# A decoder layer with split weights: which engine makes the low parts of two down-projection pieces

## The chip, the cores and the metric

The kernel runs on one core of a Trainium2 chip. A core has a matrix engine (TensorE; PE in the rows, PEld for its weight loads), three engines for elementwise work (VectorE or DVE, ScalarE or ACT, GpSimd or POOL), a queue that issues loads (SyncE or SP), and 16 DMA engines that move data between the main memory and the core's own memory. Every engine works through its own list of instructions strictly in the order in which they were written; an instruction that waits holds up all that stand behind it on its engine.

The metric is the time of one execution on the device in microseconds (us): the median of the runs.

## The reference

One layer of a hybrid decoder on 256 tokens of width 1024: attention and a convolution module side by side, an output projection with a residual sum, then a SwiGLU feed-forward block with 2816 hidden units. Only the last block matters here:

```python
h = rms_norm(x, norm2_g[l])
x = x + (jax.nn.silu(h @ w_gate[l]) * (h @ w_up[l])) @ w_down[l]
```

All numbers are float32.

## The kernel before

**Weights.** All weights come in blocks of 128 x 2048 numbers (1 MB each, `raw` in the rows), one load each, through four buffers: a block is loaded when the last reader of an earlier block has released a buffer. A block is cut into pieces of 128 x 1024. TensorE multiplies in a shorter format, so each piece is split in a high part `wh`, made by ScalarE's rounding copy (L265), and a low part `wl`, the rest. The rest is made in one of two ways (`low_part`, L213): VectorE subtracts the high part from the block (L219); or, for the pieces in the list `BY_DMA`, ScalarE copies the high part with its sign turned (L216) and GpSimd issues a DMA that adds the piece, read from main memory a second time, onto that copy (L217). The parts live in eight slots, which are reused in turn.

**Down-projection.** The 22 row blocks of `w_down` form 11 pairs, one weight block each (blocks 36 to 46). Three pairs are plain and have two pieces each, straight from the block. The other eight go through a seven-product scheme for 2 x 2 matrices: VectorE forms sums `t` of the block's quarters (three instructions, L234 to L236), three pieces are split (the first from the block, the other two from `t`), and a quarter of the block is split by itself (`single`, L255: the high half `b11h` or `other` on ScalarE at L200, the low half `b11l` or `other` on VectorE at L201). In what follows the fast pairs count from 0: sum `t4` belongs to block 41, `t5` to 42, `t6` to 44, `t7` to 45; block 43 is the plain pair with the pieces 92 and 93, block 46 the last plain pair with 100 and 101.

| block | kind | pieces |
|---|---|---|
| 42 (`t5`) | fast | 89 from the block, 90 and 91 from `t5` |
| 43 | plain | 92, 93 |
| 44 (`t6`) | fast | 94 from the block, 95 and 96 from `t6` |
| 45 (`t7`) | fast | 97 from the block, 98 and 99 from `t7` |
| 46 | plain | 100, 101 |

**Products.** TensorE (L933) takes the pairs in order. For a fast pair it multiplies three times for each of seven products: high by high, low of the other factor by high, high by low of the weight. For the pairs of `t5` and `t6` it starts with the two products on the first piece (89, 94), goes on with the one on the single quarter, and ends with those on the second and third piece. For `t7` the product on the quarter comes first and piece 97 stands near the end.

**What sets the order.** `feed(upto)` (L261) is called ahead of each group of products. It first makes the high parts of as many pieces as a look-ahead allows, in the order of the list `turns`, and then the low parts, in the order of piece numbers, of all pieces up to `upto`. `turns` sorts the pieces by number, but a piece of the table `BEHIND` stands right behind the piece named there; so it is made early, since its adding DMA takes longer. The sums `t` of a block are written in front of the first piece that needs them.

Of the kernel before, what the change touches and what calls it, by code (L numbers as in the profile page):

```python
# [61 lines left out]
FAST = [p for p in range(NF // 2) if PAIRS[p] == "F"]  # L62
PLAIN = [p for p in range(NF // 2) if PAIRS[p] == "P"]
DOWN = 72
BEHIND = {75: 70, 78: 72, 81: 75, 82: 78, 86: 80, 89: 83, 92: 86, 93: 89, 97: 92}
BY_DMA = [*range(45, DOWN, 3), *BEHIND]
FAR = 46
SUMS = {66: 0, 69: 1}
# [73 lines left out]
def _build(nc, tc, t, ctx):  # L142
# [82 lines left out]
    index = {d: DOWN + a for a, d in enumerate(down)}  # L225
    turns = sorted(range(DOWN + len(down)), key=lambda j: BEHIND[j] + 0.5 if j in BEHIND else j)
    wsums, b11 = {}, {}
# [837 lines left out]
```

## Time and profile before

| | us |
|---|---|
| median of 3 runs (291.07 to 292.76) | 291.73 |
| the profiled execution, its own time | 292.81 |
| its span, from the first instruction to the last | 291.0 |
| TensorE busy | 282.4 |
| VectorE busy | 234.9 |
| ScalarE busy | 203.5 |
| GpSimd busy | 44.4 |

The mean granted clock of TensorE was 0.994. How to read the rows of the profile further down: a row of the timeline has the start (us from the start of the span), the duration, engine, line, operation, what it writes and reads (tile numbers left out), the shapes and a count; in brackets how long its engine had been idle just before and which instruction ended that. A row of the chain has start, duration and the instruction that held the end back in that stretch. Rows of DMA issues end with the time from the issue to the landing of the data. Rows of windows have busy times by engine in a stretch of the span, then the granted clock of TensorE (PEclk, 1.00 is full), the share of DMA engines in use, and GB/s.

### The profile page before, as it was taken

The page shows a single profiled execution, that of the slowest core. Times are in us where ns is not written, and L with a number is a line of the kernel's source. Part 1 is how long each engine was busy: PE and PEld are TensorE (multiplying, and loading weights), DVE is VectorE, ACT ScalarE, POOL GpSimd, SP SyncE. Part 2 cuts the span into 40 slices and gives each one's busy share as a digit, 9 for nine tenths or more (in the row PEclk, how much of TensorE's full clock was granted, in tenths as well). Part 3 has the DMA queues.
Part 4 walks back from the last instruction along what each step waited for, and adds up shares of the span by engine and source line. Part 5 has one row for each costly group of instructions (what it writes and reads, how often), then busy time and mean ns, then how long its engine had stood idle before and what let it go on. Part 6 is the DMA issues. An engine that isn't in the chain of part 4 may idle for free.

```text
span 291.0 us, 4146 instructions
## 1 busy us (share of the span) xinstructions
PE 282.4 (97%) x1466; PEld 236.2 (81%) x1466; DVE 234.9 (81%) x419; ACT 203.5 (70%) x332; POOL 44.4 (15%) x72
## 2 busy tenths in 40 slices
PE   8999999999999999999999999999999999997695
PEld 6888877788788888888888888888888888885484
DVE  4979995895976879999967868776698899948955
ACT  5866768996639674678878767877876798854640
POOL 0005473432000000000111011111111111201042
PEclk9999999999999999999999999999999999999799
DMA  7999868647013943564999999989966699994003
GB/s 252 406 423 379 356 233 291 238 144 278 13 57 131 384 152 107 196 268 164 298 251 324 281 293 239 289 248 294 204 190 200 177 306 206 238 338 101 0 0 144
DMA packets 13062, 66.14 MB, mean 227 GB/s; under 512 B 1713, under 2 KB 2321, under 8 KB 7410
## 3 DMA queue, kind: packets, MB, share of 16 engines
q1 hardware_dynamic: 10018, 55.14, 51.9%
q0 software_dynamic: 2880, 10.74, 19.0%
q8 instruction: 11, 0.18, 0.2%
q14 instruction: 9, 0.07, 0.1%
q10 hardware_dynamic: 144, 0.00, 0.0%
HBM read 64.83 MB, written 1.05 MB: 226 GB/s over the span
## 4 chain that ended last, share of the span: by engine, by line
PE 76%; DVE 12%; ACT 5%; DMA 3%; issue 2%; ACTq 0%; DVEq 0%
PE p L709 19%; PE fg L292 12%; PE fu L292 11%; PE po L755 8%; PE fg L294 6%; PE fu L294 6%; PE sum L933 5%; ACT wh L265 4%; DVE wl L219 4%; DMA raw<-w 3%; DVE t L234 3%; PE warm L354 1%; DVE t L235 1%; PE S L543 1%; DVE t L236 1%
## 5 line engine op out<-in xcount | busy, mean ns | idle before, releaser
L265 ACT ACTIVATE wh<-raw 128x1024 fp32r<-128x1024 f32 x82 | 85.0, 1053 | 18.9 <-PE fu L292 7.8
L219 DVE TENSOR_TENSOR wl<-raw,wh 128x1024 fp32r<-128x1024 f32 x64 | 77.1, 1220 | 8.6 <-ACT wh L265 8.5
L292 PE MATMUL fu<-g,wh 128*128 128x512 f32 x176 | 62.5, 395 | 0.0
L292 PE MATMUL fg<-g,wh 128*128 128x512 f32 x176 | 62.4, 394 | 0.0
L294 PE MATMUL fg<-g,wl 128*128 128x256 f32 x176 | 48.8, 277 | 0.0
L294 PE MATMUL fu<-g,wl 128*128 128x256 f32 x176 | 48.8, 277 | 0.0
L217 POOL DMA_DIRECT2D wl<-w x18 | 15.7, 875 | 179.8 <-PE fu L294 70.5
L292 PEld LDWEIGHTS fg<-g,wh 128*128 128x128 f32 x176 | 33.0, 187 | 7.7 <-DVE g L776 0.2
L292 PEld LDWEIGHTS fu<-g,wh 128*128 128x128 f32 x176 | 33.0, 188 | 7.6
L294 PEld LDWEIGHTS fg<-g,wl 128*128 128x128 f32 x176 | 33.1, 188 | 0.0
L294 PEld LDWEIGHTS fu<-g,wl 128*128 128x128 f32 x176 | 33.1, 188 | 0.0
L933 PE MATMUL sum<-wh,forms 128*128 128x512 f32 x84 | 26.8, 401 | 0.0
L709 PE MATMUL p<-wh,xh 128*128 128x512 f32 x80 | 26.2, 409 | 0.0
L709 PE MATMUL p<-wh,xl 128*128 128x512 f32 x80 | 25.0, 394 | 0.0
L709 PE MATMUL p<-wl,xh 128*128 128x512 f32 x80 | 24.7, 390 | 0.0
L265 ACT ACTIVATE wh<-t 128x1024 fp32r<-128x1024 f32 x16 | 16.9, 1055 | 9.9 <-DVE t L234 9.1
L219 DVE TENSOR_TENSOR wl<-t,wh 128x1024 fp32r<-128x1024 f32 x16 | 19.4, 1220 | 0.2
L216 ACT ACTIVATE wl<-wh 128x1024 fp32r<-128x1024 f32 x18 | 19.1, 1062 | 0.6
L933 PEld LDWEIGHTS sum<-wh,forms 128*128 128x128 f32 x84 | 16.4, 196 | 3.5
L709 PEld LDWEIGHTS p<-wh,xl 128*128 128x128 f32 x80 | 15.3, 191 | 3.4
L709 PEld LDWEIGHTS p<-wh,xh 128*128 128x128 f32 x80 | 14.5, 191 | 4.2 <-issue 1.0
L709 PEld LDWEIGHTS p<-wl,xh 128*128 128x128 f32 x80 | 15.1, 188 | 3.3
(203 smaller groups left out, 479.7 us busy)
## 6 DMA issues: line engine op xcount, KB each, us to landing
raw<-w SPq DMA_DIRECT2D x44, 1024.0 KB, 6.4
wl<-w POOLq DMA_DIRECT2D x18, 512.0 KB, 8.2
first<-first SPq DMA_DIRECT2D x8, 384.0 KB, 5.8
raw<-w SPq DMA_DIRECT2D x2, 512.0 KB, 6.6
xtok<-xtok SPq DMA_DIRECT2D x2, 512.0 KB, 9.1
x<-xtok SPq DMA_DIRECT2D x2, 512.0 KB, 6.8
c_rows<-rows SPq DMA_DIRECT2D x1, 768.0 KB, 10.6
out<-x SPq DMA_DIRECT2D x3, 256.0 KB, 2.0
```

Of the source, the lines that this page charges most:

```text
L216: nc.scalar.activation(dst[1], dst[0].bitcast(F32), AF.Copy, scale=-1.0)
L217: nc.gpsimd.dma_start(dst[1], src.bitcast(F32R), accum_op=ALU.add)
L219: nc.vector.tensor_tensor(dst[1], src, dst[0].bitcast(F32), op=ALU.subtract)
L234: nc.vector.tensor_tensor(u[:, 0:2 * W], w[:, 0:2 * W], w[:, W:3 * W], op=ALU.add)
L235: nc.vector.tensor_tensor(u[:, 2 * W:3 * W], u[:, 0:W], w[:, 2 * W:3 * W], op=ALU.add)
L236: nc.vector.tensor_tensor(u[:, 3 * W:], u[:, 2 * W:3 * W], w[:, 3 * W:], op=ALU.add)
L265: nc.scalar.activation(dst[0], src, AF.Copy)
L292: nc.tensor.matmul(out.rearrange("p (a q) -> p a q", a=2), w[0], both, start=z in first and z not in seen, stop=False)
L294: nc.tensor.matmul(out[:, 0:T], w[1], both[:, 0, :], start=False, stop=z in last and left[z] == 0)
L709: nc.tensor.matmul(banks[i], (xh, xh, xl)[a][:, kt, sls[i]], w[a % 2], start=kt == 0 and a == 0, stop=kt == KT - 1 and a == 1)
L755: nc.tensor.matmul(po[i, n], G["mix"][l][:, k, i * P:(i + 1) * P], w[r], start=k == a == 0, stop=k == KT - 1 and a == 2)
L933: nc.tensor.matmul(banks[m], lhs, rhs, start=first, stop=last)
```

## The change

```diff
-BEHIND = {75: 70, 78: 72, 81: 75, 82: 78, 86: 80, 89: 83, 92: 86, 93: 89, 97: 92}
+BEHIND = {75: 70, 78: 72, 81: 75, 82: 78, 86: 80, 89: 83, 92: 86}
 BY_DMA = [*range(45, DOWN, 3), *BEHIND]
```

`BEHIND` has two uses, and both change for the pieces 93 and 97. They are no longer in `BY_DMA`: VectorE subtracts for them, ScalarE's two copies with the sign turned and GpSimd's two DMAs of 512 KB each are gone. And in `turns` they stand at their own numbers. The end of the list was

```
92 87 88 93 90 91 97 94 95 96 98 99 100 101
```

and is now

```
92 87 88 90 91 93 94 95 96 97 98 99 100 101
```

Three places show what that moves. Names carry their numbers here (`wh97` is the high part of piece 97, `raw45` is block 45). First ScalarE, from the step behind `wh88` to the high half of the quarter of block 44. Before:

```order
L265 ACTIVATE wh93_2724<-raw43_2602 128x1024
L216 ACTIVATE wl93_2725<-wh93_2724 128x1024
L265 ACTIVATE wh90_2735<-t5_2737 128x1024
L200 ACTIVATE other_2522<-raw42_2581 128x512
L265 ACTIVATE wh91_2753<-t5_2737 128x1024
L265 ACTIVATE wh97_2766<-raw45_2709 128x1024
L216 ACTIVATE wl97_2767<-wh97_2766 128x1024
L265 ACTIVATE wh94_2777<-raw44_2667 128x1024
L265 ACTIVATE wh95_2787<-t6_2789 128x1024
L265 ACTIVATE wh96_2804<-t6_2789 128x1024
L265 ACTIVATE wh98_2814<-t7_2816 128x1024
L200 ACTIVATE b11h_1077<-raw44_2667 128x512
```

The same place now:

```order
L265 ACTIVATE wh90_2724<-t5_2726 128x1024
L265 ACTIVATE wh91_2738<-t5_2726 128x1024
L200 ACTIVATE other_2522<-raw42_2581 128x512
L265 ACTIVATE wh93_2752<-raw43_2602 128x1024
L265 ACTIVATE wh94_2764<-raw44_2667 128x1024
L265 ACTIVATE wh95_2774<-t6_2776 128x1024
L265 ACTIVATE wh96_2788<-t6_2776 128x1024
L265 ACTIVATE wh97_2801<-raw45_2709 128x1024
L265 ACTIVATE wh98_2811<-t7_2813 128x1024
L200 ACTIVATE b11h_1077<-raw44_2667 128x512
```

The high part of 97, which reads block 45, stood in front of those of 94, 95 and 96, which read block 44; it stands behind them now. The high part of 91 has moved in front of the high half of the quarter (`other`).

Second VectorE, behind the sum `t5`. Before:

```order
L219 TENSOR_TENSOR wl90_2736<-t5_2737,wh90_2735 128x1024
L201 TENSOR_TENSOR other_2522<-raw42_2581,other_2522 128x512
L219 TENSOR_TENSOR wl91_2754<-t5_2737,wh91_2753 128x1024
L219 TENSOR_TENSOR wl94_2778<-raw44_2667,wh94_2777 128x1024
L234 TENSOR_TENSOR t6_2789<-raw44_2667 128x1024
```

The same place now:

```order
L219 TENSOR_TENSOR wl90_2725<-t5_2726,wh90_2724 128x1024
L219 TENSOR_TENSOR wl91_2739<-t5_2726,wh91_2738 128x1024
L201 TENSOR_TENSOR other_2522<-raw42_2581,other_2522 128x512
L219 TENSOR_TENSOR wl93_2753<-raw43_2602,wh93_2752 128x1024
L234 TENSOR_TENSOR t6_2776<-raw44_2667 128x1024
```

The low half of the quarter of block 42 stands behind the low part of 91 now, and the low part of 93 has come in between. The low part of 94 has gone behind the sum `t6`.

Third VectorE, from the low part of 96 on. Before:

```order
L219 TENSOR_TENSOR wl96_2805<-t6_2789,wh96_2804 128x1024
L234 TENSOR_TENSOR t7_2816<-raw45_2709 128x1024
L235 TENSOR_TENSOR t7_2816<-t7_2816,raw45_2709 128x512
L236 TENSOR_TENSOR t7_2816<-t7_2816,raw45_2709 128x512
L201 TENSOR_TENSOR b11l_1078<-raw44_2667,b11h_1077 128x512
L219 TENSOR_TENSOR wl98_2815<-t7_2816,wh98_2814 128x1024
```

The same place now:

```order
L219 TENSOR_TENSOR wl96_2789<-t6_2776,wh96_2788 128x1024
L234 TENSOR_TENSOR t7_2813<-raw45_2709 128x1024
L235 TENSOR_TENSOR t7_2813<-t7_2813,raw45_2709 128x512
L236 TENSOR_TENSOR t7_2813<-t7_2813,raw45_2709 128x512
L219 TENSOR_TENSOR wl97_2802<-raw45_2709,wh97_2801 128x1024
L201 TENSOR_TENSOR b11l_1078<-raw44_2667,b11h_1077 128x512
```

The low part of 97 has come in ahead of the low half of the quarter of block 44 (`b11l`). TensorE's products stand in the same order as before. One more thing follows from the two DMAs: the load of block 46 waited for ScalarE (the last reader of block 43, the high part of 93), and now waits for VectorE (the last reader of block 42, the low half of its quarter).

## The prediction

> **What bounds the kernel now.** I read the page first, for the engine that is nearest to the whole span; then TensorE's timeline for its gaps; then the chain of waits, backwards from the largest gap.
>
> ```profile
> PE 282.4 (97%) x1466; PEld 236.2 (81%) x1466; DVE 234.9 (81%) x419; ACT 203.5 (70%) x332; POOL 44.4 (15%) x72
> ```
>
> TensorE is busy for 97% of the span, and its matmuls are the same before and after. So the change can only act through the few stretches in which TensorE waits or runs slowly. The timeline has one:
>
> ```profile
> 257.07 0.84 PE L933 MATMUL sum<-other,forms 128*128 128x512 f32 x3
> 257.75 0.62 PE L933 MATMUL sum<-wh,forms 128*128 128x512 f32 x2
> ...
> 267.14 0.39 PE L933 MATMUL sum<-wl,forms 128*128 128x512 f32 x1
> 272.09 1.00 PE L933 MATMUL sum<-b11h,forms 128*128 128x512 f32 x2 [4.56 <-ACT b11h L200]
> 272.89 0.72 PE L933 MATMUL sum<-b11l,forms 128*128 128x512 f32 x1
> ...
> 277.28 0.84 PE L933 MATMUL sum<-other 128*128 128x512 f32 x3
> ...
> 282.04 0.62 PE L933 MATMUL sum<-wh,act 128*128 128x512 f32 x2
> ```
>
> Three matmuls from 257.07 to 257.75 give a slot of 0.227 us each at full speed. After 267.14 the next could start at 267.37; it starts at 272.09, because the quarter of block 44 (`b11h`, `b11l`) was not split: 4.72 us lost. And the 15 matmuls from 272.09 to 277.28 take 5.19 us in place of 15 x 0.227 = 3.41, so 1.78 more. The second loss has its reason in the granted clock:
>
> ```profile
> 272.00:275.50 3.50, 3.41 (x8) 2.45 (x9) 3.43 (x4) 3.40 (x5) 0.00 (x0) 0.55 0.00 0
> 275.50:287.00 11.50, 11.50 (x55) 9.63 (x54) 7.78 (x11) 3.50 (x5) 5.12 (x4) 0.99 0.08 29
> ```
>
> 0.55 behind the gap, 0.99 afterwards. Together the place costs 6.50 us. The chain says what held it:
>
> ```profile
> 251.57 8.22 DMA raw<-w
> ...
> 259.88 1.07 ACT wh L265
> ...
> 261.94 1.05 ACT wh L265
> ...
> 263.01 1.23 DVE wl L219
> ...
> 268.01 1.23 DVE wl L219
> ...
> 270.46 1.06 ACT wh L265
> 271.52 0.53 ACT b11h L200
> ...
> 272.09 14.19 PE sum L933 x54
> ```
>
> The load issued at 251.57 is block 45 (it follows the release of block 41). ScalarE's next instruction needs it:
>
> ```profile
> 253.91 1.06 ACT L265 ACTIVATE wh<-t 128x1024 fp32r<-128x1024 f32 x1 [0.89 <-DVE t L234]
> 254.88 0.61 ACT L200 ACTIVATE other<-raw 128x512 fp32r<-128x512 f32 x1
> 255.40 1.05 ACT L265 ACTIVATE wh<-t 128x1024 fp32r<-128x1024 f32 x1
> 259.88 1.06 ACT L265 ACTIVATE wh<-raw 128x1024 fp32r<-128x1024 f32 x1 [3.44 <-DMA raw<-w]
> 261.94 1.04 ACT L265 ACTIVATE wh<-raw 128x1024 fp32r<-128x1024 f32 x1
> ```
>
> By the order shown above these are `wh90`, `other`, `wh91`, `wh97`, and, behind `wl97`, `wh94`. Piece 97 is multiplied near the very end, yet its high part stands in front of that of 94, so everything on block 44 waits for block 45. Block 44 itself was there:
>
> ```profile
> raw<-w SPq DMA_DIRECT2D x1, 1024.0 KB, 6.3
> ...
> raw<-w SPq DMA_DIRECT2D x1, 1024.0 KB, 8.2
> ...
> raw<-w SPq DMA_DIRECT2D x1, 1024.0 KB, 11.8
> ```
>
> These are the last three loads: block 44, issued at 247.25, landed 6.3 us later, at 253.6; block 45 at 259.8; block 46, issued at 252.0, at 263.8. VectorE meanwhile:
>
> ```profile
> 254.58 0.69 DVE L236 TENSOR_TENSOR t<-t,raw 128x512 f32<-128x512 f32 x1
> 255.19 1.22 DVE L219 TENSOR_TENSOR wl<-t,wh 128x1024 fp32r<-128x1024 f32 x1
> 256.32 0.68 DVE L201 TENSOR_TENSOR other<-raw,other 128x512 fp32r<-128x512 f32 x1
> ...
> 263.01 1.23 DVE L219 TENSOR_TENSOR wl<-raw,wh 128x1024 fp32r<-128x1024 f32 x1 [4.87 <-ACT wh L265]
> 264.15 1.22 DVE L234 TENSOR_TENSOR t<-raw 128x1024 f32<-128x1024 f32 x1
> 265.41 0.69 DVE L235 TENSOR_TENSOR t<-t,raw 128x512 f32<-128x512 f32 x1
> 266.13 0.69 DVE L236 TENSOR_TENSOR t<-t,raw 128x512 f32<-128x512 f32 x1
> 266.74 2.49 DVE L219 TENSOR_TENSOR wl<-t,wh 128x1024 fp32r<-128x1024 f32 x2
> ...
> 272.07 0.69 DVE L201 TENSOR_TENSOR b11l<-raw,b11h 128x512 fp32r<-128x512 f32 x1 [0.25 <-ACT b11h L200]
> 272.68 2.35 DVE L219 TENSOR_TENSOR wl<-t,wh 128x1024 fp32r<-128x1024 f32 x2
> ```
>
> It sat idle for 4.87 us, until 263.01, waiting for `wh94`; ahead of that it had no gap from 254.58 on.
>
> **The change part by part.** Removed: two sign-turned copies on ScalarE (which idles here anyway, so nothing), two DMA issues on GpSimd (nothing else stands there until the last sums), and 1 MB of reads. Fewer reads can only bring block 45 sooner than 259.8, and I use no gain from that. Added: two subtractions on VectorE, 1.14 us each from start to start (263.01 to 264.15). Up to 254.58 nothing moves. From there I lay VectorE out anew by its own spacings, start to start: a subtraction L219 1.14; the sum's thirds 1.26, 0.72 and 0.61; a quarter L201 0.61 (272.07 to 272.68).
>
> - `wl90` at 255.19 as before. `wh91` needs the last third of `t5`, done at 255.27; it started at 255.40 before, behind `other`, and can start at 255.4 now, ahead of it; it ends at 256.4. `wl91` runs from 256.45. The high half `other` follows `wh91` (0.5 behind it), at 256.9. The low half then runs from 257.59 to 258.28.
> - Here is the price. TensorE needs that low half for the third of the matmuls at 257.07, due at 257.52. Data made by VectorE reaches TensorE 0.13 later (`b11l` ends at 272.76, the matmul starts at 272.89), so it starts at 258.41: **0.9 us** lost, and all of TensorE's work behind it is 0.9 later.
> - `wl93` at 258.20; TensorE needs it at about 264. `t6` at 259.34, 260.60, 261.32; block 44 has been there since 253.6. `wl94` at 261.93, `wl95` 263.07, `wl96` 264.21. Their high parts have been made on ScalarE by then: `wh93` and `wh94` directly behind `other`, `wh95` after the first third of `t6`, `wh96` by 263.1.
> - `t7` at 265.35, 266.61, 267.33; block 45 has been there since 259.8 at the latest. `wl97` at 267.94. `b11l` from 269.08 to 269.77. On ScalarE `wh98` follows the first third of `t7` (ends at 266.57) and `b11h` follows that, done at 268.2.
> - TensorE comes to the quarter of block 44 at 267.37 + 0.90 = 268.27. `b11h` is ready; the third matmul, due at 268.72, waits for `b11l` until 269.90: **1.18 us** lost. It ends its slot at 270.13, and 12 matmuls of 0.227 later, at 272.85, stands what stood at 277.28.
> - Behind that: `wl98` 269.69, `wl99` 270.83, the low half of block 45's quarter from 271.97 to 272.66, needed at 272.85 + 2 x 0.227 = 273.3; `wl100` and `wl101` are done at 274.9, needed at 282.04 - 4.4 = 277.6. So no new wait, and the rest of the span moves as a whole.
>
> The stall of 6.50 goes; what is late next is VectorE itself, with 0.90 + 1.18 = 2.08. The sum is 6.50 - 2.08 = **4.4 us** less. The profiled execution took 292.81, and would take 288.4. It was 1.1 above the median of the runs; from the median, 291.73 - 4.4 = **287.3 us**.
>
> Unknown in this is what TensorE's clock does after two stalls of 0.9 and 1.2 us; no stall of that length inside the work stands in the trace. The bounds are nothing (the only drop there is follows 4.56 us of idling) and the whole 1.78 again. I take nothing, because both stalls together are under half of the one gap that shows a drop, and TensorE works for 10 us between them. [...]
>
> The load of block 46 is issued later, after 258.28 in place of 252.0. With 6.3 to 11.8 us it lands between 264.6 and 270.1. ScalarE takes it up for `wh100` behind `wh99`, at about 269.1, so at the worst ScalarE is 1.0 late; the high half of block 45's quarter, next on ScalarE, is then done at 271.7, still before 272.85. I cost it at nothing; both ends of its range give nothing.
>
> **The rivals.**
>
> - *The clock falls anyway.* Each short stall, or the two together, brings the slow stretch back: 287.3 + 1.8 = 289.1. For it: the stalls come in the same place. Against it: their length.
> - *The wait only moves, block 45 is the bound.* `t7` needs block 45 at 265.35, and `wh97` at about 263.1. Each us that it lands beyond 265.35 is an us on the path; the gain is used up at 269.8, which is 18.2 us after its issue. That gives 291.7. Against it: 8.2 us in the trace, with more traffic around it than there will be.
> - *Block 46 comes too late, and the time is longer than before.* ScalarE's `wh100` stands ahead of the high half of block 45's quarter, so its wait would be passed on to TensorE just as `wh97` did. The half needs 1.6 us behind the landing, TensorE wants it at 272.85: it decides from a landing at 271.2, 12.9 us after its issue. For 0.5% slower than before it has to land 6 us later still. At 20 us after its issue (278.3) the time would be 287.3 + 7.1 = 294.4. For it: it is issued 6 us later and the kernel's longest of the three was 11.8. Against it: that one had block 45's and piece 93's transfers beside it.
> - *The change does nothing of the kind* because pieces 93 and 97 still come by DMA: the orders above rule that out.
>
> **How the numbers follow.** Forecast 0.68, 287.3, with 286.4 (the 0.9 at block 42's quarter stays hidden) to 288.2 as its own range. The clock 0.13, at 289.1. Block 45: 0.05. Block 46: 0.05. The remaining 0.09 is for waits that I do not see, most of which would cost part of the gain. The range is 286.3 to 289.6: it takes in the forecast and the clock's rival and leaves out about 0.15. About 0.5% (1.5 us) is what a measurement of this kernel can tell from no change. Faster by more than that holds the first two and most of the rest, 0.87; within it 0.07; slower 0.06.
>
> **What would show it.** In the profile after: no gap of ScalarE that block 45's load ends; VectorE without a gap from about 251 to 274; TensorE with two waits, about 0.9 us at some 257.5 for `other` and about 1.2 us at some 268.7 for `b11l`, in place of 4.56; a granted clock of 1.00 through 265 to 278; the last group `sum<-other` near 272.9. The forecast is wrong if the clock falls behind one of the waits, if a load ends a wait of ScalarE beyond 265, or if VectorE's row of subtractions has gaps that I have not laid out.

## The result, and the profile after

| kernel | median us | range, executions |
|---|---|---|
| before | 291.73 | 291.07 to 292.76, 5 |
| changed | 288.47 | 288.29 to 290.19, 5 |

The ratio of the changed kernel's time to that of before is 0.9895, with a 95% interval from 0.986 to 0.9931: faster by about 1.1%. The profiled execution took 288.62 us with a span of 286.8; that of before 292.81 and 291.0. So the two profiled executions are 4.2 us apart, the medians 3.3.

TensorE's row of the profile's page has hardly moved, since its work is the same:

```profile
PE 281.2 (98%) x1466; PEld 235.1 (82%) x1466; DVE 236.8 (83%) x421; ACT 201.5 (70%) x330; POOL 42.6 (15%) x70
```

The timeline of TensorE in the changed kernel, at the quarter of block 42, at that of block 44 and at that of block 45:

```profile
257.18 0.66 PE L933 MATMUL sum<-other,forms 128*128 128x512 f32 x2
258.45 0.50 PE L933 MATMUL sum<-other,forms 128*128 128x512 f32 x1 [0.61 <-DVE other L201]
...
268.40 0.73 PE L933 MATMUL sum<-b11h,forms 128*128 128x512 f32 x2
269.90 0.50 PE L933 MATMUL sum<-b11l,forms 128*128 128x512 f32 x1 [0.77 <-DVE b11l L201]
...
272.98 0.84 PE L933 MATMUL sum<-other 128*128 128x512 f32 x3
```

The gap of 4.56 us is gone; two short waits for VectorE have come. A slot is the 0.227 us from one matmul to the next at a granted clock of 1.00 (three of them from 257.07 to 257.75 in the profile of before). The third matmul on block 42's quarter was due at 257.18 + 2 x 0.227 = 257.63 and starts at 258.45, 0.82 late. The third on block 44's was due at 268.85 and starts at 269.90, 1.05 late. The bracket gives less, since it counts from the end of the matmul before and not from the slot. Block 45's quarter comes at 272.98, where it came at 277.28.

ScalarE in the changed kernel:

```profile
255.47 1.06 ACT L265 ACTIVATE wh<-t 128x1024 fp32r<-128x1024 f32 x1 [0.39 <-DVE t L236]
256.44 0.62 ACT L200 ACTIVATE other<-raw 128x512 fp32r<-128x512 f32 x1
256.95 1.99 ACT L265 ACTIVATE wh<-raw 128x1024 fp32r<-128x1024 f32 x2
260.78 1.06 ACT L265 ACTIVATE wh<-t 128x1024 fp32r<-128x1024 f32 x1 [1.83 <-DVE t L234]
...
267.74 0.61 ACT L200 ACTIVATE b11h<-raw 128x512 fp32r<-128x512 f32 x1
```

Behind the high part of 91 and `other` come the high parts of 93 and 94 in one row, from 256.95; no load ends a wait here. In these rows ScalarE waits for VectorE. VectorE has no gap:

```profile
255.29 2.50 DVE L219 TENSOR_TENSOR wl<-t,wh 128x1024 fp32r<-128x1024 f32 x2
257.71 0.68 DVE L201 TENSOR_TENSOR other<-raw,other 128x512 fp32r<-128x512 f32 x1
258.31 1.22 DVE L219 TENSOR_TENSOR wl<-raw,wh 128x1024 fp32r<-128x1024 f32 x1
...
268.03 1.22 DVE L219 TENSOR_TENSOR wl<-raw,wh 128x1024 fp32r<-128x1024 f32 x1
269.16 0.68 DVE L201 TENSOR_TENSOR b11l<-raw,b11h 128x512 fp32r<-128x512 f32 x1
```

These are the low parts of 90 and 91, the low half of block 42's quarter, the low part of 93, and, ten microseconds later, the low part of 97 and the low half of block 44's quarter. The windows show what the clock did around the second wait:

```profile
268.50:272.00 3.50, 2.73 (x11) 1.96 (x12) 3.50 (x4) 3.22 (x4) 0.00 (x0) 1.00 0.00 0
272.00:275.50 3.50, 3.50 (x18) 2.88 (x17) 2.99 (x4) 1.32 (x2) 0.14 (x1) 1.00 0.00 0
```

The granted clock is 1.00 in both, where the kernel before had 0.55 from 272.00 to 275.50.

### The profile page after: what moved, and what is told of

Its sections match the earlier page's. It is cut to its first block, busy times and chain, and to the rows that moved or that the text cites. A ratio compares the mean times of both kernels' runs of the same rounds, so it can differ in the third digit from the quotient of the medians.

```text
span 286.8 us, 4144 instructions
## 1 busy us (share of the span) xinstructions
PE 281.2 (98%) x1466; PEld 235.1 (82%) x1466; DVE 236.8 (83%) x421; ACT 201.5 (70%) x330; POOL 42.6 (15%) x70
## 3 DMA queue, kind: packets, MB, share of 16 engines
HBM read 63.79 MB, written 1.05 MB: 226 GB/s over the span
## 4 chain that ended last, share of the span: by engine, by line
PE 78%; DVE 14%; ACT 4%; issue 3%; ACTq 0%; DVEq 0%
PE p L709 20%; PE fg L292 12%; PE fu L292 12%; PE po L755 8%; PE fg L294 6%; PE fu L294 6%; PE sum L933 5%; DVE wl L219 5%; ACT wh L265 3%; DVE t L234 3%; DVE t L235 1%; PE warm L354 1%; PE S L543 1%; DVE t L236 1%; PE pT L573 1%
## 5 line engine op out<-in xcount | busy, mean ns | idle before, releaser
L219 DVE TENSOR_TENSOR wl<-raw,wh 128x1024 fp32r<-128x1024 f32 x66 | 79.6, 1219 | 3.7 <-ACT wh L265 3.7
L217 POOL DMA_DIRECT2D wl<-w x16 | 14.0, 875 | 167.5 <-PE fu L294 70.5
L933 PE MATMUL sum<-wh,forms 128*128 128x512 f32 x84 | 25.9, 389 | 0.0
L933 PEld LDWEIGHTS sum<-wh,forms 128*128 128x128 f32 x84 | 15.7, 188 | 3.2
L216 ACT ACTIVATE wl<-wh 128x1024 fp32r<-128x1024 f32 x16 | 17.0, 1062 | 0.5
```

Source lines behind the costliest of these rows:

```text
L216: nc.scalar.activation(dst[1], dst[0].bitcast(F32), AF.Copy, scale=-1.0)
L217: nc.gpsimd.dma_start(dst[1], src.bitcast(F32R), accum_op=ALU.add)
L219: nc.vector.tensor_tensor(dst[1], src, dst[0].bitcast(F32), op=ALU.subtract)
L933: nc.tensor.matmul(banks[m], lhs, rhs, start=first, stop=last)
```

## Experiments

Two theories stood. **Place**: what cost the time was the place of 97's high part in ScalarE's list, ahead of those of block 44; that the low parts went over to VectorE brought nothing and costs VectorE's time, which shows as the two new waits. **Traffic**: the two DMAs less made the loads land sooner. The change does both at once, so the first four runs do one part each; they ran on one chip, beside the kernel before, which took 293.44 there (291.34 to 295.38). Each ratio is to the kernel before on the same chip, with its 95% interval in brackets.

### The place alone: 97 keeps its DMA

```diff
-BEHIND = {75: 70, 78: 72, 81: 75, 82: 78, 86: 80, 89: 83, 92: 86, 93: 89, 97: 92}
+BEHIND = {75: 70, 78: 72, 81: 75, 82: 78, 86: 80, 89: 83, 92: 86, 93: 89, 97: 96}
```

> Piece 97 keeps its adding DMA and loses only its early place: its high part stands behind that of 96 (93 as before). If the place in ScalarE's list made the gain, the 4.56 us gap goes here too, and since VectorE has neither subtraction to make, the two new stalls of 0.6 and 0.8 us are absent: 1.5 to 2.5 us faster than the changed kernel, 285.5 to 287.0. If the two DMAs less made the gain, all nine are still there: 291 to 292, like before.

Measured: 286.22 (285.90 to 286.53, 6 executions), ratio to before 0.978 [0.9746, 0.9815]. TensorE's timeline:

```profile
256.67 0.84 PE L933 MATMUL sum<-other,forms 128*128 128x512 f32 x3
...
266.87 0.61 PE L933 MATMUL sum<-b11h,forms 128*128 128x512 f32 x2
267.32 0.47 PE L933 MATMUL sum<-b11l,forms 128*128 128x512 f32 x1
...
270.37 0.84 PE L933 MATMUL sum<-other 128*128 128x512 f32 x3
```

No wait of 0.1 us is left at either quarter. With all nine DMAs of `BEHIND` kept, the whole gain is there and, by the medians, 2.2 us more than in the changed kernel. The place theory holds; this version beats both kernels.

### The DMAs alone: old places, VectorE subtracts

```diff
-BY_DMA = [*range(45, DOWN, 3), *BEHIND]
+BY_DMA = [j for j in [*range(45, DOWN, 3), *BEHIND] if j not in (93, 97)]
```

> The two DMAs are gone as in the changed kernel, VectorE subtracts, but both high parts keep their early places, that of 97 in front of that of 94. Place theory: ScalarE still waits for block 45 until about 259.5 and TensorE still has a gap of 3 to 4 us for block 44's quarter; what is saved is one copy on ScalarE (1.06), what is added is one subtraction ahead of b11l (1.14): 290.5 to 292. Traffic theory: 288 to 289, like the changed kernel.

Measured: 291.76 (289.75 to 293.84, 12 executions), ratio 0.9961 [0.9929, 0.9993]. ScalarE, then TensorE at the quarters of blocks 42 and 44:

```profile
258.43 2.01 ACT L265 ACTIVATE wh<-raw 128x1024 fp32r<-128x1024 f32 x2 [2.17 <-DMA raw<-w]
```

```profile
256.89 0.84 PE L933 MATMUL sum<-other,forms 128*128 128x512 f32 x3
...
269.57 0.73 PE L933 MATMUL sum<-b11h,forms 128*128 128x512 f32 x2 [2.32 <-ACT b11h L200]
271.07 0.50 PE L933 MATMUL sum<-b11l,forms 128*128 128x512 f32 x1 [0.76 <-DVE b11l L201]
```

The wait for block 45 is there and ends at 258.43, where it ended at 259.88 in the profile of before. The whole run gains 0.4%, about a third of the change's 1.1%. The gap ahead of block 44's quarter is 2.3 us long; the low half then adds a second wait, so that the third matmul, due at 267.54, starts at 271.07, 3.5 late in all, within the 3 to 4 that I expected. Whether less traffic made the load land sooner is not shown. Block 45's load took 7.0 us here; it took 7.4 to 8.8 in the four profiles with all nine DMAs, and 6.9 and 7.7 in the two of the changed kernel, which makes the same seven as this run, so the two groups overlap. ScalarE also saves the copy of 1.06 us between the high parts of 97 and 94, and no run separates the two. What follows: the DMAs are at most a small part, and they play no part in the changed kernel through block 45, since nothing waits for it there.

### One piece at a time

```diff
-BEHIND = {75: 70, 78: 72, 81: 75, 82: 78, 86: 80, 89: 83, 92: 86, 93: 89, 97: 92}
+BEHIND = {75: 70, 78: 72, 81: 75, 82: 78, 86: 80, 89: 83, 92: 86, 97: 92}
```

> Only 93 goes to VectorE; 97 keeps DMA and its place behind 92, and so stands ahead of the high parts of 93 and 94. Place theory: ScalarE waits for block 45 with 93 behind it too; gap for block 44's quarter as long as before or up to 1 us longer: 291.5 to 293. Traffic theory (512 KB less): 290 to 291.

Measured: 294.12 (291.90 to 295.30, 12 executions), ratio 1.0026 [0.9995, 1.0058]: no gain; as a time it is above what I had written, most likely because the kernel before took longer on this chip too. ScalarE, then TensorE:

```profile
259.42 1.06 ACT L265 ACTIVATE wh<-raw 128x1024 fp32r<-128x1024 f32 x1 [2.89 <-DMA raw<-w]
260.51 1.06 ACT L216 ACTIVATE wl<-wh 128x1024 fp32r<-128x1024 f32 x1
261.47 2.00 ACT L265 ACTIVATE wh<-raw 128x1024 fp32r<-128x1024 f32 x2
```

```profile
257.93 0.50 PE L933 MATMUL sum<-other,forms 128*128 128x512 f32 x1 [0.60 <-DVE other L201]
...
272.76 1.22 PE L933 MATMUL sum<-b11h,forms 128*128 128x512 f32 x2 [4.80 <-ACT b11h L200]
```

Now 93 and 94 both stand behind 97, and the gap is 4.80. The wait at block 42's quarter is there as well. The other half:

```diff
-BEHIND = {75: 70, 78: 72, 81: 75, 82: 78, 86: 80, 89: 83, 92: 86, 93: 89, 97: 92}
+BEHIND = {75: 70, 78: 72, 81: 75, 82: 78, 86: 80, 89: 83, 92: 86, 93: 89}
```

> Only 97 goes to VectorE and to its own place; 93 keeps its DMA. Place theory: no wait of ScalarE for block 45; the low half of block 42's quarter is ahead of the low part of 91 again, so no 0.6 us stall there, and one subtraction (97) is ahead of b11l, a stall of about 0.8 us at most: 286.5 to 288, i.e. up to 1.5 us faster than the changed kernel. Traffic theory: half the gain, about 290.

Measured: 287.34 (286.81 to 287.50, 6 executions), ratio 0.9814 [0.9782, 0.9846], with one wait of TensorE:

```profile
267.31 0.61 PE L933 MATMUL sum<-b11h,forms 128*128 128x512 f32 x2
268.51 0.50 PE L933 MATMUL sum<-b11l,forms 128*128 128x512 f32 x1 [0.59 <-DVE b11l L201]
```

All of the gain hangs on 97. And the three medians stand in a row: 286.22 with neither subtraction, 287.34 with that of 97, 288.47 with both (this one not from the same chip; 288.45 when repeated on another). By the medians each subtraction on VectorE costs 1.1 us; one takes 1.14 from start to start.

But it is not one wait for each subtraction. The wait at block 42's quarter comes from the order of `wl91` and the low half of the quarter, which goes with the place of 93. With 93 alone it is there (257.93), though the subtraction for 93 stands behind it; without the two DMAs, where both subtractions are made but the places are the old ones, it is absent (256.89, three matmuls in a row). Nor does it add to the total, as far as the rows tell: in the changed kernel VectorE works without a gap until `b11l` is done, so had TensorE not waited at block 42's quarter, it would have waited that much longer there. No run makes both subtractions with 97 in its new place and 93 in its old one, so this last step is argued.

### How much of block 44 has to go ahead

```diff
-BEHIND = {75: 70, 78: 72, 81: 75, 82: 78, 86: 80, 89: 83, 92: 86, 93: 89, 97: 92}
+BEHIND = {75: 70, 78: 72, 81: 75, 82: 78, 86: 80, 89: 83, 92: 86, 93: 89, 97: 94}
```

> All nine DMAs; piece 97 stands behind the high part of 94 and ahead of those of 95 and 96, halfway between before and the run with its place alone changed. Place theory: ScalarE waits for block 45 until 259.5 to 260 with 95 and 96 behind it, the sum for block 45 comes at about 265.3, the quarter of block 44 is done about 1 us after TensorE wants it: 0.7 to 1.3 us slower than with 97 behind 96, so 286.9 to 287.6, with no drop of the clock. If only being ahead of 94 matters: 286.2, as there.

Measured: 287.30 (286.47 to 289.81, 6 executions), ratio 0.9858 [0.9807, 0.9909], on another chip (before: 292.54, 290.16 to 295.49). The median is inside what the place theory gave, partly by luck, as is shown below. ScalarE:

```profile
256.43 1.04 ACT L265 ACTIVATE wh<-raw 128x1024 fp32r<-128x1024 f32 x1
259.10 1.06 ACT L265 ACTIVATE wh<-raw 128x1024 fp32r<-128x1024 f32 x1 [1.62 <-DMA raw<-w]
```

The high part of 94 is made at 256.43, that of 97 waits for its load, and those of 95 and 96 wait with it. A miss is in it: two of the six executions took 289.8 at a mean clock of 0.992 and 0.993, where I had ruled a drop out. In the profiled one the quarter of block 44 was only about 0.3 us late, where I had expected 1 us; what it was in those two is not shown. The other four took 286.47 to 287.62, so the two long ones lift the median.

### The kernels of before and after once more

Both unchanged, on the chip of the run above.

> The kernel before, unchanged, for another profile and the clock of every execution. If the time that the change took away is a wait for a load, it differs from execution to execution: the span of a profile is 284.1 (the span with the place of 97 changed alone) plus the gap ahead of block 44's quarter and what the lower clock costs behind it, within 0.7 us. The executions spread over 2 us or more, against 0.7 for the kernels without that wait.

> The changed kernel, unchanged, beside the others of this call. Place theory: 288.3 to 288.8 as before, whatever the kernel before takes on this chip, with two stalls of about 0.6 and 0.8 us. If both kernels simply run slower on one chip than on another, it moves by the same share as the kernel before.

The changed kernel: 288.45 (288.03 to 288.71, 6 executions), ratio 0.9877 [0.9838, 0.9915]. It is where it was, while the kernel before went from 291.73 to 293.44, 292.54 and, in its own row, 292.96 (290.50 to 295.51, 12 executions). The profile of the kernel before in this run has a span of 290.3, and this place in TensorE's timeline:

```profile
266.84 0.39 PE L933 MATMUL sum<-wl,forms 128*128 128x512 f32 x1
271.16 0.73 PE L933 MATMUL sum<-b11h,forms 128*128 128x512 f32 x2 [3.93 <-ACT b11h L200]
...
276.54 0.85 PE L933 MATMUL sum<-other 128*128 128x512 f32 x3
```

From 267.07, when the matmul was due, to 271.16 are 4.09; the 15 matmuls to 276.54 take 5.38 in place of 3.41. Together 6.06, and with the 284.1 of the place alone and 0.2 by which this execution is later at block 42's quarter (256.87 against 256.67) 290.4: the span, within 0.1. The first profile of the kernel before closes in the same way: 284.1, its stall of 6.50, and 0.4 by which it is later at block 42's quarter (257.07) make 291.0, its span. So in both profiles the difference to the kernel with 97's place changed is this one place and next to nothing else.

## Why the prediction was right, and what was off

- **The bound.** One wait of ScalarE for block 45 with block 44's work behind it: right. It goes when 97 alone is moved, and stays when only the DMAs go.
- **The price.** Forecast 0.90 and 1.18, together 2.08. Measured 0.82 and 1.05 at the two matmuls, with some 0.3 beside them (the pair on `b11h` 0.08 late, the slots of the two late matmuls 0.1 longer each). From block 42's quarter to block 45's the changed kernel takes 15.80 us (257.18 to 272.98) and the one with 97's place alone 13.70 (256.67 to 270.37): 2.10 more. In medians the two subtractions cost 2.2. One step does not follow: the lower end of the forecast's own range, 286.4, lets the first 0.9 stay hidden and takes it off the sum. By the prediction's own layout VectorE has no gap up to `b11l`, so TensorE would have waited 0.9 longer there.
- **The sum.** Block 45's quarter was forecast at 272.85 and came at 272.98; this execution was 0.11 later already at 257. The profiled execution was forecast at 288.4 and took 288.62. The median of 288.47 lies inside the stated range, but 0.3 above the forecast's own, which ended at 288.2.
- **From the profile to the median: this term was mis-sized.** The prediction took 4.4 off the median of 291.73 and said 287.3; the median is 288.47, 3.3 off. The step supposed that an execution 1.1 us over the median is slower all along. But the time of the kernel before varies at the very place that the change removes. Of its 52 executions with a clock on record, 3 had a mean clock of 0.998 or more and took 290.2 to 290.5; 21 had about 0.993 and took 291.3 to 293.8; 28 had about 0.987 and took 292.5 to 295.5. The changed kernel was within 288.0 to 288.7 in ten of eleven executions. The 1.1 us of the profiled one most likely belonged to the stall (its own sum, 291.0 above, has all of its surplus over the kernel with 97's place changed in the stall but for 0.4; the executions at that median have no profile), and then had to go with it: 292.81 - 4.4 = 288.4 was the better forecast for the median too.
- **Rivals.** The clock stayed at 0.997 or more in all eleven executions, so the short waits did not bring it down here. That part is right with some luck: the reason given was the waits' length beside a gap of 4.56 us, but in the run without the two DMAs waits of 2.32 and 0.76 us were enough, and how near the changed kernel is to that was not tried. Block 45 landed at about 259.4, needed first at 263.2 by the high part of 97 and at 265.4 by the sum `t7`. Block 46, the rival on the slow side, was issued at about 258.4 and landed 5.4 later, at 263.8; ScalarE took it at 269.2. The loads of blocks 44, 45 and 46 in the changed kernel, size and time to landing:

```profile
raw<-w SPq DMA_DIRECT2D x1, 1024.0 KB, 6.8
...
raw<-w SPq DMA_DIRECT2D x1, 1024.0 KB, 7.7
...
raw<-w SPq DMA_DIRECT2D x1, 1024.0 KB, 5.4
```

One thing stays open: one of the changed kernel's executions took 290.19 at a clock of 0.999. It was not profiled, and no run says why.

## What to carry to other kernels

Where an engine works strictly in order, ask of every step that is made early what it waits for and who stands behind it: a step taken forward for a slow transfer held up a whole block that had long landed (ScalarE stood until 259.88 for block 45, while block 44 had been there since 253.6). A change that moves work and changes its place is to be taken apart: here the place was worth 6.5 us by the ratio (0.978 of 293.44; the two medians are 7.2 apart) and the moved work cost 2.2. And a profile's surplus over the median need not be spread over the span; look first whether the wait in question is the part that varies.

## What the runs showed of the hardware

In the run without the two DMAs the granted clock fell behind gaps shorter than the 4.56 us of before. TensorE stood for 2.32 us, worked, and stood for 0.76 us; then the clock went from 1.00 to 0.50, with TensorE at work again since 271.07. The windows of that run (the third number from the end is the granted clock):

```profile
271.00:271.50 0.50, 0.43 (x2) 0.39 (x3) 0.50 (x2) 0.50 (x2) 0.00 (x0) 1.00 0.00 0
271.50:272.00 0.50, 0.50 (x4) 0.41 (x3) 0.50 (x1) 0.50 (x2) 0.00 (x0) 0.91 0.00 0
272.00:272.50 0.50, 0.50 (x3) 0.41 (x2) 0.50 (x2) 0.50 (x1) 0.00 (x0) 0.50 0.00 0
...
275.00:276.00 1.00, 1.00 (x6) 0.78 (x5) 1.00 (x2) 0.00 (x0) 0.00 (x0) 0.84 0.00 0
```

If it is 0.50 all the while it is down, 0.91 puts the fall at 271.9 and 0.84 the return at 275.3, by my estimate 3.4 us. In the run with 93 alone it fell while TensorE still stood (until 272.76), and stayed down for twice as long:

```profile
270.00:271.00 1.00, 0.00 (x0) 0.00 (x0) 1.00 (x1) 0.00 (x0) 0.00 (x0) 0.84 0.00 0
...
277.00:278.00 1.00, 1.00 (x4) 0.80 (x4) 1.00 (x2) 0.00 (x0) 0.00 (x0) 0.74 0.00 0
```

By the same working from 270.7 to 277.5, 6.8 us. The two lengths fit the three groups of the kernel before: 0.993 of some 290 us is 2 us of clock lost (3.4 at half is 1.7), 0.987 is 3.8 (6.8 at half is 3.4). That is an estimate from the mean clocks; most of those executions have no profile.

In the run without the two DMAs no wait of TensorE was longer than 2.32 us, and the clock fell all the same; why it fell there, no run shows. In the 3.4 us ahead of that fall (268.5 to 271.9, as long as it then stayed down) TensorE was busy for 1.56 us; in the changed kernel it was busy for 2.63 of the 3.4 us from 268.0 to 271.4, with the longer of its two waits inside, and the clock stayed at 1.00. What the clock does with waits between the changed kernel's two (0.6 and 0.8 us idle, ten microseconds apart) and that run's 2.3 and 0.8 was not tried.
